# Another build-time order of the experts' steps in a two-block layer

## The chip, the cores and the metric

The kernel runs on one core of one Trainium2 chip. Times are device microseconds (us) of an execution; the median of three runs of the kernel before is 3551.99 us (3551.24 to 3552.19).

## The reference

`reference()` computes two transformer-like blocks one after the other on 1024 tokens of width 1024. The first has two linear-attention scans, and then a mixture of experts; the second has four mixers, a feed-forward layer and a gated projection. Only the mixture of experts matters here:

```python
def hier_moe(h, rg_w, rg_b, re_w, re_b, e_w_in, e_w_out):
    ...
    g_idx = jnp.argmax(g_logits, axis=-1)
    ...
    top_v, top_i = lax.top_k(e_in_group, TOP_K)
    weights = g_w * jax.nn.softmax(top_v, axis=-1)
    ...
    def expert_block(args):
        xb, e = args
        gate, up = jnp.split(xb @ e_w_in[e], 2, axis=-1)
        return (jax.nn.silu(gate) * up) @ e_w_out[e]
    ...
    y = yb[dest] * weights.reshape(-1)[order][:, None].astype(yb.dtype)
    out = jax.ops.segment_sum(y, token_of, num_segments=t)
```

32 experts share 2048 assignments of tokens. Each expert's weights are 6 MB in float32, 201 MB in all, and each is read once.

## The kernel before, in words

The routing sorts the experts by how many tokens they have got; what the program calls expert 0 is the one with most, up to 28, and the numbers 29 to 31 are three fixed experts. BLOCKS (line 21) gives each its blocks of rows: expert 0 has 128, 128, 128 and 64 rows, expert 1 has 128, 128 and 64, expert 2 has 128 and 64 (these three are the split experts), experts 3 to 7 have one block of 128 rows, 8 to 17 and 29 one of 64, and 18 to 28, 30 and 31 one of 32. There are 38 blocks. An expert's weights come in 12 chunks of 128 x 1024 (512 KB): eight for the first product, four for the second.

The blocks are shared out between two streams. The first stream has the list MANY (line 26). Its experts 0 to 7 use the fast float32r matmul with weights split in a high and a low part: a chunk is loaded into one of four places (tile `eraw`), split by ScalarE and VectorE into `ehi` and `elo` (`split`, lines 232 and 233) with twelve places each, and used by `block` (128 rows, six matmuls of 128 x 512 for each chunk, line 246) or `block_packed` (64 rows, line 1310). The weights of experts 30 and 29 are loaded ahead into the places of `ehi` and `elo`. The second stream has the list FEW (line 27): its chunks are loaded into one of ten places (tile `ew`) and used as they are, by `block_plain` (64 rows, lines 1358 to 1374) or `block_small` (32 rows, line 1399). Each block begins with a gather of its rows by GpSimd (`xg`, line 1238), a transposition by TensorE, and ends with a scatter (`y2d`, line 1427). Between the products ScalarE and VectorE compute silu and the product (`ga`), and their transposition (`ah`).

`blocks()` is a generator: for each step (a transposition, or the matmuls of one chunk or of two) it yields the planner's own length, the pause until the stream's next step can start, the chunks that the step needs, the expert, and whether this is the expert's last block. `run_experts()` is a planner that runs while the program is built. It keeps a time `t`, a bus on which a chunk takes TWELFTH and lands LANDING later, and for both streams the time at which their next step could start; it picks one step, lets the generator write its instructions, and goes on. When a step of an expert's last block has used its chunks, a place is free: for the second stream the next chunk's load is issued, for the first the place goes to a list and the next raw chunk that has landed is split into it, whereupon the next raw chunk is loaded. So the picks fix the order of all instructions of the stage on each engine, and the order of the loads on the DMA queue of SyncE, through which the 350 loads of the stage go (96 `eraw`, 254 `ew`; 34 more chunks are loaded ahead of it). At the end the order on each engine is made binding. In the kernel before a step of the second stream is taken if it can start no later than the first stream's, 0.05 us of play included. After the experts follow a loop for blocks that don't fit (zero passes here), and the next stage, which reads the scattered rows back from `y2d`.

Of the kernel before, what the change touches and what calls it, by code (L numbers as in the profile page):

```python
# [22 lines left out]
NB = sum(len(b) for b in BLOCKS)  # L23
NT = 64

MANY = (30, 29, 0, 1, 2, 3, 4, 5, 6, 7)
FEW = (31,) + tuple(range(8, 29))

PLACES = {"ew": 10, "ehi": 12, "elo": 12, "eraw": 4}
TWELFTH, LANDING = 1.45, 1.5  # L30

FIRST = (8, 10, 0, 12, 14, 4, -1, 1, 5, -2, 2, 6, 3, 7)

# [137 lines left out]
class Kern:  # L171
# [1295 lines left out]
    def run_experts(self, streams, orders, W, pools):  # L1467

        nc, tc = self.nc, self.tc
        cur = nc.cur_bb.bb
        first = len(cur.instructions)
        number, src = {}, lambda i, c: number[i](c)
        queue = [[(i, c) for i in o for c in range(12) if (i, c) not in W] for o in orders]
        there = {k: 0.0 for k in W}
        free, raws = [], []
        t, bus, cut, ready = 0.0, 0.0, 0.0, [0.0, 0.0]  # L1480

        def load(s):
            nonlocal bus
            if not queue[s]:
                return
            i, c = queue[s].pop(0)
            if i not in number:
                number[i] = self.expert(self.place(i))
            if s:
                w = W[i, c] = pools[1].tile([128, 1024], F32, tag="ew", name="ew", bufs=PLACES["ew"])  # L1490
                nc.sync.dma_start(w, src(i, c))
            else:
                w = pools[0].tile([128, 1024], F32, tag="eraw", name="eraw", bufs=PLACES["eraw"])
                nc.sync.dma_start(w, src(i, c))
            bus = max(t, bus) + TWELFTH
            if s:
                there[i, c] = bus + LANDING
            else:
                raws.append((i, c, w, bus + LANDING))

        def splits(now):

            nonlocal cut
            while raws and free and max(raws[0][3], free[0], cut) <= now:
                i, c, raw, at = raws.pop(0)
                cut = max(at, free.pop(0), cut) + 1.3
                hi, lo = [pools[0].tile([128, 1024], F32R, tag=n, name=n, bufs=PLACES[n]) for n in ("ehi", "elo")]
                self.split(hi, lo, raw)
                W[i, c] = hi, lo
                there[i, c] = cut + 1.3  # L1510
                load(0)

        for _ in range(PLACES["eraw"]):
            load(0)
        steps = [next(s, None) for s in streams]
        while any(steps):
            splits(t)
            at = [max([t, ready[s]] + [there.get((p[3], c), 1e9) for c in p[2]]) if p else 1e9 for s, p in enumerate(steps)]
            s = int(at[1] <= at[0] + 0.05)
            if at[s] > t + 0.25:  # L1520
                t += 0.2
                continue
            length, pause, cs, i, last = steps[s]
            t = max(t, at[s]) + length
            ready[s] = t + pause
            steps[s] = next(streams[s], None)
            for c in cs if last else ():
                if s == 1:
                    load(1)
                elif i < 8 or c % 2:  # L1530
                    free.append(t)
        assert not raws and not queue[0] and not queue[1]

        before = {}
        for ins in cur.instructions[first:]:
            if ins.engine in before:
                tc.add_manual_dep(ins, before[ins.engine], mybir.DependencyInfo(mybir.DependencyClass.NoSync, mybir.DependencyReason.DATA),
                                  reason="order of the experts")
            before[ins.engine] = ins.name

    def moe(self):
        nc, I, tc = self.nc, self.I, self.tc
        self.y2d = self.dr.tile([2048, 1024], F32, name="y2d")
        with ExitStack() as es:
            with ExitStack() as e1:
# [7 lines left out]
                with ExitStack() as e2:  # L1553
                    self.banks(e2, p=4)
                    self.route(self.pool(e2, "route", 1))
                    for e in (30, 29):
# [4 lines left out]
                self.tap("ord", self.ord)  # L1561
                streams = [self.blocks(pl, 1, [(i, j) for i in MANY for j in range(len(BLOCKS[i]))], W, "128"),
                           self.blocks(sm, 2, [(i, 0) for i in FEW], W, "64")]
                self.run_experts(streams, (MANY, FEW), W, (wp, sp))

# [819 lines left out]
```

## Time and profile before

| what | value |
|---|---|
| median of three runs | 3551.99 us |
| profiled execution, time | 3553.5 us |
| profiled execution, span | 3551.6 us |
| TensorE busy | 3315.7 us, 93% of the span |
| VectorE busy | 1836.0 us, 52% |
| ScalarE busy | 1141.1 us, 32% |
| GpSimd busy | 274.5 us, 8% |
| moved by DMA | 527.49 MB, 149 GB/s on the mean |
| mean granted clock of TensorE | 0.961 |

How to read it: the experts' stage lies from 805 us (the first load that the planner issues) to 1411 us. PE is TensorE, PEld its weight load, DVE VectorE, ACT ScalarE, POOL GpSimd, SP SyncE; L1399 is line 1399 of the kernel. A busy share that is an average over the span says little of one stage, so the rows below are of this stage. The granted clock is in parts of full speed.

### The profile page before, as it was taken

What the parts mean: (1) busy time and instruction counts of PE and PEld (TensorE: products, weight loads), DVE (VectorE), ACT (ScalarE), POOL (GpSimd) and SP (SyncE); (2) the same over time, 40 slices, a digit from 0 to 9 for tenths busy, and PEclk for the clock granted to TensorE, in tenths of its full rate; (3) what the DMA queues carried; (4) which work ended last, traced back from release to release, by engine and by line L of the source; (5) the groups of instructions that cost most, each with busy time, mean ns of one, the idle gap of its engine ahead of it and who ended that gap; (6) DMA issues with size and microseconds to landing.
All of it is one profiled execution on the core that took longest, in us unless ns stands there. A gap on an engine that the chain in (4) does not pass through costs nothing.

```text
span 3551.6 us, 42850 instructions
## 1 busy us (share of the span) xinstructions
PE 3315.7 (93%) x15995; PEld 2498.7 (70%) x15995; DVE 1836.0 (52%) x3311; ACT 1141.1 (32%) x2003; POOL 274.5 (8%) x246
## 2 busy tenths in 40 slices
PE   7999988986998886699999999999999999999998
PEld 4887767872444444477778777777787888888876
DVE  7846565773123455832355544556755444444455
ACT  2423242432112344522275223334314222212224
POOL 4001022002111110410000000000000000000000
PEclk8999978997999998799999999999999999999999
DMA  4234536359999986622221333324631111111122
GB/s 173 88 110 149 181 111 200 125 215 354 358 358 355 383 334 212 239 93 100 96 68 58 117 116 112 101 84 143 234 122 61 55 48 48 52 54 50 36 72 78
DMA packets 211723, 527.49 MB, mean 149 GB/s; under 512 B 22476, under 2 KB 72208, under 8 KB 209592
## 3 DMA queue, kind: packets, MB, share of 16 engines
q1 hardware_dynamic: 203704, 503.74, 40.1%
q0 software_dynamic: 6656, 16.79, 1.3%
q10 hardware_dynamic: 1152, 4.19, 0.3%
q8 instruction: 127, 2.08, 0.2%
q14 instruction: 84, 0.69, 0.1%
HBM read 445.43 MB, written 84.62 MB: 149 GB/s over the span
## 4 chain that ended last, share of the span: by engine, by line
PE 58%; DMA 3%; DVE 2%; ACT 1%; issue 1%; SPq 0%; POOL 0%; DVEq 0%; POOLq 0%; ACTq 0%
PE pd L239 8%; PE pd L240 8%; PE pd L238 8%; PE pg L238 5%; PE pg L239 5%; PE pg L240 5%; PE pp L239 3%; PE pp L240 3%; PE pp L238 3%; PE pS L1870 2%; PE po L1907 1%; DMA eraw<-in_ew 1%; PE pt L1894 1%; PE pg L246 1%; PE py L246 1%
## 5 line engine op out<-in xcount | busy, mean ns | idle before, releaser
L239 PE MATMUL pd<-H,thi 128*128 128x512 f32 x896 | 350.9, 392 | 0.5 <-DVE H L1649 0.5
L238 PE MATMUL pd<-H,thi 128*128 128x512 f32 x896 | 350.9, 392 | 0.1
L240 PE MATMUL pd<-H,tlo 128*128 128x512 f32 x896 | 350.7, 392 | 0.0
L232 ACT ACTIVATE thi<-traw 128x1024 fp32r<-128x1024 f32 (+3 forms) x145 | 132.5, 917 | 518.6 <-PE pd L239 319.0
L2257 DVE TENSOR_TENSOR M<-M,pp 128x512 f32<-128x512 f32 x256 | 173.8, 685 | 233.4 <-PE pp L240 232.4
L233 DVE TENSOR_TENSOR tlo<-traw,thi 128x1024 fp32r<-128x1024 f32 (+3 forms) x145 | 151.0, 1045 | 175.4 <-ACT thi L232 175.3
L238 PE MATMUL pg<-H,thi 128*128 128x512 f32 x512 | 209.4, 409 | 0.0
L240 PE MATMUL pg<-H,tlo 128*128 128x512 f32 x512 | 208.2, 407 | 0.0
L239 PE MATMUL pg<-H,thi 128*128 128x512 f32 x512 | 207.8, 406 | 0.0
L239 PE MATMUL pp<-flo,hh 128*128 128x512 f32 x512 | 199.2, 389 | 0.5 <-DVE flo L233 0.5
L238 PE MATMUL pp<-fhi,hh 128*128 128x512 f32 x512 | 199.4, 390 | 0.0
L239 PEld LDWEIGHTS pd<-H,thi 128*128 128x128 f32 x896 | 168.2, 188 | 41.7 <-issue 5.8
L238 PEld LDWEIGHTS pd<-H,thi 128*128 128x128 f32 x896 | 168.2, 188 | 39.0 <-issue 2.2
L240 PEld LDWEIGHTS pd<-H,tlo 128*128 128x128 f32 x896 | 168.2, 188 | 38.8 <-issue 4.3
L240 PE MATMUL pp<-fhi,hl 128*128 128x512 f32 x512 | 194.7, 389 | 0.0
L238 PE MATMUL pd<-nhi,mh 128*128 128x512 f32 x384 | 154.6, 404 | 4.5 <-ACT nhi L232 3.5
L239 PE MATMUL pd<-nlo,mh 128*128 128x512 f32 x384 | 153.1, 399 | 1.1 <-DVE nlo L233 1.1
L240 PE MATMUL pd<-nhi,ml 128*128 128x512 f32 x384 | 150.4, 401 | 0.0
L233 DVE TENSOR_TENSOR elo<-eraw,ehi 128x1024 fp32r<-128x1024 f32 x96 | 115.1, 1223 | 40.3 <-ACT ehi L232 39.2
L238 PEld LDWEIGHTS pg<-H,thi 128*128 128x128 f32 x512 | 96.4, 188 | 30.6 <-issue 9.6
L240 PEld LDWEIGHTS pg<-H,tlo 128*128 128x128 f32 x512 | 96.4, 188 | 25.9 <-issue 4.8
L239 PEld LDWEIGHTS pg<-H,thi 128*128 128x128 f32 x512 | 96.3, 188 | 25.6 <-issue 5.3
(764 smaller groups left out, 7156.6 us busy)
## 6 DMA issues: line engine op xcount, KB each, us to landing
ew<-in_ew SPq DMA_DIRECT2D x264, 512.0 KB
eraw<-in_ew SPq DMA_DIRECT2D x96, 512.0 KB
traw<-in_w2T SPq DMA_DIRECT2D x56, 512.0 KB
ada<-in_ada SPq DMA_DIRECT2D x64, 256.0 KB
gd<-sg SPq DMA_DIRECT2D x64, 256.0 KB
sg<-gd SPq DMA_DIRECT2D x64, 256.0 KB
traw<-in_ff1T SPq DMA_DIRECT2D x32, 512.0 KB
fraw<-in_ff SPq DMA_DIRECT2D x32, 512.0 KB
```

The source lines that it names most:

```text
L232: self.nc.scalar.activation(hi, src, AF.Copy)
L233: (eng or self.nc.vector).tensor_tensor(lo, src, hi.bitcast(F32), op=OP.subtract)
L238: mm(out, L[0], R[0], start=start, stop=False)
L239: mm(out, L[0], R[1], start=False, stop=False)
L240: mm(out, L[1], R[0], start=False, stop=stop)
L246: self.nc.tensor.matmul(out[j], L[a], R[b][:, j * 512:j * 512 + 512], start=start and i == 0, stop=stop and i == 2)
L1870: nc.tensor.matmul(p[:, :w], q[:, i * 128:i * 128 + 128], k[:, b * 512:b * 512 + w], start=True, stop=True)
L1894: nc.tensor.transpose(pt[:, j * 128:j * 128 + 128], P[:, jj * 128:jj * 128 + 128], self.ident)
L1907: nc.tensor.matmul(po[h * 64:h * 64 + 64, ii * 128:ii * 128 + 128], self.av[:, j, hh * 64:hh * 64 + 64], PT[:, j], start=(j == 0), stop=(j ...
L2257: nc.vector.tensor_tensor(X[:, t, c], X[:, t, c], p, op=OP.add)
```

## The change

The order of both lists changes: MANY now takes the large experts in the order 3, 0, 4, 5, 1, 6, 2, 7 and FEW takes a 64-row and a 32-row expert in turn. Where both streams' next steps can start within 0.05 us of each other, the first stream goes first if its step belongs to an expert's last block, otherwise the second; apart from that the earlier one goes, where the play of 0.05 us favoured the second stream. In the planner's own reckoning a step takes 1.08 of its length and a pause 1.15 of its own. The blocks, their instructions and their weights stay as they are.

```diff
--- before.py
+++ after.py
@@ -23,11 +23,12 @@
 NB = sum(len(b) for b in BLOCKS)
 NT = 64
 
-MANY = (30, 29, 0, 1, 2, 3, 4, 5, 6, 7)
-FEW = (31,) + tuple(range(8, 29))
+MANY = (30, 29, 3, 0, 4, 5, 1, 6, 2, 7)
+FEW = (31, 8, 18, 9, 19, 10, 20, 11, 21, 12, 22, 13, 23, 14, 24, 15, 25, 16, 26, 17, 27, 28)
+
 
 PLACES = {"ew": 10, "ehi": 12, "elo": 12, "eraw": 4}
-TWELFTH, LANDING = 1.45, 1.5
+TWELFTH, LANDING, SLOW = 1.45, 1.5, (1.08, 1.15)
 
 FIRST = (8, 10, 0, 12, 14, 4, -1, 1, 5, -2, 2, 6, 3, 7)
 
@@ -1470,6 +1471,7 @@
 
 
 
+
         nc, tc = self.nc, self.tc
         cur = nc.cur_bb.bb
         first = len(cur.instructions)
@@ -1516,13 +1518,15 @@
         while any(steps):
             splits(t)
             at = [max([t, ready[s]] + [there.get((p[3], c), 1e9) for c in p[2]]) if p else 1e9 for s, p in enumerate(steps)]
-            s = int(at[1] <= at[0] + 0.05)
+            s = int(at[1] < at[0])
+            if abs(at[1] - at[0]) < 0.05:
+                s = 1 - int(steps[0][4])
             if at[s] > t + 0.25:
                 t += 0.2
                 continue
             length, pause, cs, i, last = steps[s]
-            t = max(t, at[s]) + length
-            ready[s] = t + pause
+            t = max(t, at[s]) + length * SLOW[0]
+            ready[s] = t + pause * SLOW[1]
             steps[s] = next(streams[s], None)
             for c in cs if last else ():
                 if s == 1:
```

## Rows read from the trace of the kernel before

**Rows 1.** Page, part 2: 40 slices, TensorE's busy tenths and GB/s
```profile
PE   7999988986998886699999999999999999999998
GB/s 173 88 110 149 181 111 200 125 215 354 358 358 355 383 334 212 239 93 100 96 68 58 117 116 112 101 84 143 234 122 61 55 48 48 52 54 50 36 72 78
```

**Rows 2.** Stretches: us, busy us of five engines, TensorE's clock, DMA share, GB/s
```profile
820.00:1300.00 480.00, 426.56 (x2203) 213.90 (x2202) 163.02 (x218) 131.77 (x197) 71.40 (x66) 0.94 0.96 364
1300.00:1381.00 81.00, 55.44 (x230) 36.57 (x229) 53.36 (x54) 45.02 (x51) 8.98 (x6) 0.87 0.78 271
1381.00:1411.00 30.00, 26.02 (x103) 19.48 (x101) 8.77 (x10) 7.37 (x10) 2.00 (x1) 0.91 0.30 100
1300.00:1411.00 111.00, 81.46 (x331) 56.05 (x329) 62.13 (x64) 52.38 (x61) 10.98 (x7) 0.88 0.65 225
818.00:1411.00 593.00, 509.47 (x2544) 271.43 (x2544) 225.15 (x282) 184.54 (x258) 82.52 (x73) 0.93 0.90 337
```

**Rows 3.** SyncE's DMA queue: start, us, line, operation, out<-in, how many
```profile
804.92 4.05 SPq L1494 DMA_DIRECT2D eraw<-in_ew  x4
...
1298.26 0.91 SPq L1491 DMA_DIRECT2D ew<-in_ew  x2
1299.41 81.72 SPq L1494 DMA_DIRECT2D eraw<-in_ew  x39
```

**Rows 4.** The chain of waits near the end of the stage: start, us, what
```profile
1368.06 1.07 ACT ehi L232
1369.15 1.24 DVE elo L233
1370.40 5.10 DMA eraw<-in_ew
```

**Rows 5.** TensorE's waits, 1300 to 1411 us: us in total, times, longest
```profile
PE py L1277 <- DVE ga L1273: 10.6, 4, 5.7
PE py L246 <- ACT ah L232: 7.1, 3, 3.8
```

**Rows 6.** The page's third part, the queue of GpSimd's gathers and scatters
```profile
q0 software_dynamic: 6656, 16.79, 1.3%
```

**Rows 7.** Timeline of several engines, first and last pieces of the stage
```profile
818.55 1.88 PE L1390 MATMUL py<-ident,xg 32*128 32x32 f32 x16 [10.59 <-DMA xg<-h2d,gidx]
...
1304.56 1.06 PE L1399 MATMUL pg<-ew,xh 128*32 128x512 f32 x8
...
1310.79 3.14 PE L1399 MATMUL pg<-ew,ah 128*32 128x512 f32 x16 [1.81 <-DVE ah L1418]
1314.60 1.37 DVE L1423 TENSOR_TENSOR ey<-od,pg 32x512 f32<-32x512 f32 x2 [3.86 <-ACT od L1405]
...
1392.95 0.33 SPq L1673 DMA_DIRECT2D cx<-x1d  x1
...
1409.47 0.61 PE L246 MATMUL py<-ehi,al 128*128 128x512 f32 x2
1411.57 0.99 POOL L1427 DMA_INDIRECT y2d<-ey,sidx  x1 [21.91 <-DVEq L1573]
...
1432.72 1.97 PE L1643 MATMUL pp<-ident,cb 128*128 128x128 f32 x8 [22.63 <-DMA traw<-in_w2T]
```

**Rows 8.** A stretch of 20 us, the one with most traffic
```profile
1080.00:1100.00 20.00, 19.39 (x108) 11.05 (x108) 9.15 (x12) 7.61 (x11) 4.76 (x4) 1.00 1.03 410
```

**Rows 9.** Stretch of the tile ehi alone: ACT's count is the splits
```profile
820.00:1300.00 480.00, 158.27 (x478) 81.76 (x479) 66.84 (x56) 56.76 (x56) 0.94 0.96 364
```

**Rows 10.** TensorE's waits for split weights, 820 to 1300 us
```profile
PE pg L246 <- ACT ehi L232: 5.4, 3, 3.2
PE pg L246 <- DVE elo L233: 1.5, 3, 0.6
PE py L246 <- ACT ehi L232: 1.4, 1, 1.4
```

## The prediction

> **What bounds the kernel now.** I read the 40 slices of the page first [rows 1]. Two things stand beside each other from slice 10 to slice 15: the memory traffic is at its highest of the whole span (about 355 GB/s), and TensorE is nearly full too. That is the experts' stage, the only part that the change touches. So I next took the table of stretches for this stage [rows 2]. From 820 to 1300 us TensorE is busy for 426.56 of 480 us (0.889) while the DMA engines are busy at 0.96 and move 364 GB/s: both are close to full at once, and neither can give much. From 1300 to 1381 us both drop, TensorE to 55.44 of 81 us and the traffic to 271 GB/s; from 1381 to 1411 the traffic is 100 GB/s. The stage therefore has a long good part and 111 us of a poor end.
>
> The DMA queue of SyncE says why [rows 3]. The last weights of the second stream (FEW) are issued at 1298.26 us. From 1299.41 us on, 39 loads of the first stream (MANY) follow alone, and they need 81.72 us, 2.10 us each. Before that, 350 - 39 = 311 loads went out between 804.92 and 1299 us, 1.588 us each. A lone first stream is slow because each of its chunks is a chain of its own: the chain of waits shows a load, then a split on ScalarE (1.07 us), then one on VectorE (1.24 us), then the next load [rows 4], with four places for raw chunks. TensorE meanwhile waits for gated and transposed activations that stand behind those splits in the queues of ScalarE and VectorE, 10.6 + 7.1 us in this stretch [rows 5].
>
> **What the change does to the order.** The kernel's planner runs while the program is built, and its rule is short enough to be followed step by step. I used only the order that it gives, not its times. For the kernel before, the order ends with 39 raw loads in a row, which is just what the trace has [rows 3], so the rule is read rightly. With the new lists, tie rule and factors the same walk gives: expert 30 starts ahead of 31; the last raw load is number 340 of 350 and ten direct loads follow; expert 7 (the last of MANY) does its second product just after the first step of expert 28, the last of FEW, and the last seven steps of the stage are those of expert 28, a 32-row block; the last two loads, its own chunks, are issued when the first of these seven has freed two places. Before, 46 steps of the first stream followed the last step of the second; now none. Loads, matmuls, splits, gathers and scatters stay the same in number and size; only their order on each engine's queue, and on SyncE's, changes. The longest run of direct loads stays about as long (102 before, 100 now).
>
> **The sum.** Two terms carry it, and both lie on the path that sets the end of the stage.
> First, the 39 loads move into the mixed part. At its pace they cost 39 x 1.588 = 62 us, where they now take 81.7: 20 us less. Hence the last load goes out at 1299 + 62 = 1361 us. The same from the bytes: 350 loads of 0.524 MB are 183.5 MB, the gathers and scatters 16.8 MB [rows 6], together 200.3 MB; at 364 GB/s that is 550 us from 805, or 1355 us. The first is taken.
> Second, what follows the last load. Now a whole 128-row block does: the last load is issued at 1381.1 us and TensorE ends at 1410.1 us [rows 7], 29 us later. Afterwards it is the rest of a 32-row block: two steps of 1.06 us, and then what lies between the start of its fourth step at 1304.56 and the end of its last at 1313.93 us in expert 28 of the kernel before [rows 7], 9.4 us: 11.5 us in all. The landing (some 5 us by the last load's wait in the chain [rows 4]) is hidden under that. This is 17.5 us less, and TensorE ends near 1372.5 us.
> Against this, the 32-row block's way from TensorE to the scatter is ScalarE's od and two VectorE additions, which end 2.0 us after the matmuls, and then the issue; after the 128-row block the whole way was 1.5 us [rows 7]: about 1 us more. The next stage's TensorE start at 1432.72 [rows 7] hangs on weights issued behind the reading of the scattered rows, so it follows this end. Four prefetches of the next stage (the first at 1392.95 us [rows 7]) stand behind the experts' loads on SyncE; they were hidden under expert 7 and will be issued some 11 us ahead of the end. If that cover fails I allow 5 us, if the smaller scatter lands sooner -2 us, and I take zero, since the stage waits for the scatter anyhow. Starting with expert 30 in place of 31 is taken at zero: both wait for gathers issued one after the other, and the DMA engines are full there anyhow.
> The sum is -20 - 17.5 + 1 = -36.5 us. The profiled execution has a span of 3551.6 us and took 3553.5, 1.5 us above the median of the runs, 3551.99; so the median goes to 3515.
>
> **What could make it otherwise.**
> *TensorE sets the pace.* The new order needs TensorE's 509.47 us of this stage [rows 2] within 554 us, a share of 0.920, above the 0.889 of the good part. If it can't pass 0.889, the stage takes 509.47 / 0.889 = 573 us from 818.5 [rows 7] and ends at 1391, 19 us sooner than now: 3533. For it speaks that the good part holds idle time of TensorE (53 us) which mixing needn't remove; against it, that 509 us contain work at the lower clock (granted mean 0.88 from 1300 to 1411 against 0.94 before [rows 2]) which a fuller queue would shorten. A rule speaks against this rival: the Trainium skill, "Perfetto Trace Analysis", Identifying the Most-Contended Engine, holds that matmul busy time says little of how near TensorE is to its limit, and weight-load busy time more. By that, TensorE was loaded to only 213.90 of 480 us [rows 2], this rival would drop out, and the first sum would stand alone. I keep it, because the same rows show 53 us of open time and no more in which further matmuls could have started.
>
> *Both get better.* If the mixing holds places of both streams open all the time, the traffic could stay at the 410 GB/s that single stretches of 20 us show [rows 8]: 200.3 MB would need 489 us, and TensorE becomes the limit. With half of the good part's idle time gone it ends at 818.5 + 509 + 27 = 1354, -56 us: 3496. Against this the Trainium skill, "DMA: Bandwidth & Descriptors", Where 436 GB/s comes from, takes about 358 GB/s as what binds a core's transfers from HBM. By that figure, as an estimate, 200.3 MB need 560 us, the last byte lands at 1365 us and the sum stays near its -36. The stretch at 410 doesn't agree with such a bound; the mean of 364 does, so this rival keeps a small chance.
>
> *The splits hold up both streams (the other side).* All engines work their queue in order. The 40 splits that lie in the poor end now, where only their own stream suffers, move among the matmuls' evacuations of both streams: of 96 splits, 56 were in the good part [rows 9]. In the poor end TensorE stood idle 111 - 81.5 = 29.5 us beside 40 splits, 0.74 us each; in the good part its waits for split weights, 5.4 + 1.5 + 1.4 us [rows 10], make 0.15 us each for 56. If a split costs 0.74 us everywhere, TensorE needs 818 + 509 + 45 (the 53 us without those waits) + 96 x 0.74 = 1443 us, 33 us later than now: 3585. The point of no gain is at 0.40 us a split (38 us spare over 96), and the loss passes 0.2% from 0.47 us. For it: new ties go to the first stream, whose chunks come last. Against it: 0.15 us is what rows of mixed work show.
>
> *No change that can be told.* A split cost between those bounds, 0.33 to 0.47 us, or a tail that lengthens elsewhere by some 35 us. 3552.
>
> **How the numbers follow.** The DMA pace with the short tail, -36.5 us, has 0.45 (its own range 3504 to 3527: the byte sum's 6 us and as much again for loads that pack better on the one side; 5 us for the prefetches and 6 for a tail at the lower clock on the other). TensorE's pace, -19: 0.25. Both better, -56: 0.15. No change within 0.2% (7 us, about what a measurement can tell): 0.08. Slower through the splits: 0.07. So faster has 0.85, same 0.08, slower 0.07. The range leaves out the last two and a part of the best case, and reaches from -62 to -12 us: 3490 to 3540.
>
> **What would show it.** In the profile of the changed kernel the issues of both streams should end within some 15 us of each other, near 1361 us; no run of 39 raw loads; the last matmuls of the stage of the 32-row form, near 1372 us; the traffic at 355 to 375 GB/s up to the end, and TensorE above 0.9 busy. The first term is wrong if loads go out slower than 1.588 us each; the second, if another block ends last. If TensorE's waits for split weights come to more than 0.40 us a split, the other side was right; if TensorE stays below 0.9 while loads wait for places, its pace was the bound.

## The result, and the profile after

The changed kernel takes 3497.07 us (median of four runs, 3495.09 to 3499.05) where the kernel before takes 3552.09 us: a ratio of 0.9844, with a 95% interval of 0.9827 to 0.9861. That is 55 us sooner; the forecast was 37 us, with 3490 to 3540 as its range. The profiled execution has a span of 3493.3 us, 58.3 us less than that of before. Lines behind the edit have moved by one to four in `kernel.py`: line 1399 of before is 1400, 246 is 247, 1494 is 1496 and 1643 is 1647.

The page's slices, which answer to [rows 1]:

```profile
PE   7999988996998995899999999999999999999998
GB/s 176 78 111 154 187 93 212 121 186 341 382 389 378 397 383 281 181 97 97 76 79 64 121 136 91 95 82 190 201 109 73 49 49 49 49 51 49 33 73 79
```

The stretches of the experts' stage, to be held against [rows 2] (us, busy us of PE, PEld, DVE, ACT and POOL with counts, the granted clock, the DMA engines' share, GB/s):

```profile
820.00:1300.00 480.00, 436.67 (x2252) 233.44 (x2244) 197.16 (x245) 162.04 (x224) 69.97 (x64) 0.98 0.99 378
1300.00:1360.00 60.00, 49.62 (x272) 29.61 (x272) 27.46 (x36) 23.10 (x34) 6.74 (x7) 0.95 0.83 317
818.00:1360.00 542.00, 488.30 (x2531) 263.67 (x2529) 224.62 (x281) 185.53 (x258) 77.62 (x72) 0.97 0.97 370
```

The good part has become better and longer at once: 378 GB/s instead of 364 from 820 to 1300 us, and no poor end of 111 us behind it. All matmuls of the stage together are busy for 488.30 us instead of 509.47, since they run at the full clock more of the time (granted mean 0.97 instead of 0.93).

SyncE's queue at the end of the stage, which answers to [rows 3] (start, us, queue, line, operation, out<-in, how many):

```profile
1320.55 0.33 SPq L1496 DMA_DIRECT2D eraw<-in_ew  x1
1324.42 16.47 SPq L1493 DMA_DIRECT2D ew<-in_ew  x8
...
1349.06 0.93 SPq L1493 DMA_DIRECT2D ew<-in_ew  x2
...
1350.57 12.96 SPq L271 DMA_DIRECT2D nraw<-in_w2z  x2
```

The last raw load goes out at 1320.55 us and ten direct loads follow, as the walk through the planner's rule said. But the streams' last issues lie 28.5 us apart, where the prediction looked for some 15, and the traffic falls to 317 GB/s in the last 60 us, where it looked for 355 to 375 up to the end. TensorE's last pieces, which answer to [rows 7]:

```profile
1347.97 3.64 PE L1400 MATMUL pg<-ew,xh 128*32 128x512 f32 x32
1354.49 0.63 PE L1417 MATMUL py<-ident,ga 32*128 32x32 f32 x4 [2.88 <-DVE ga L1413]
1355.51 3.64 PE L1400 MATMUL pg<-ew,ah 128*32 128x512 f32 x16 [0.38 <-DVE cnt L1575]
1384.45 1.97 PE L1647 MATMUL pp<-ident,cb 128*128 128x128 f32 x8 [25.30 <-DVE cb L1713]
```

The stage ends with expert 28 at 1359.15 us, 51 us sooner. Split up, with the ends of the rows shown:

| stretch of the profiled execution | before, us | after, us | difference | forecast |
|---|---|---|---|---|
| up to the stage's first load | 804.9 | 803.8 | -1.1 | 0 |
| first load to the last load's issue | 576.2 | 546.2 | -30.0 | -20 |
| last load's issue to the experts' last matmul | 29.0 | 9.2 | -19.8 | -17.5 |
| to the next stage's first transposition | 22.6 | 25.3 | +2.7 | +1 |
| to line 1820 (1824 after), the first `av` | 148.2 | 139.8 | -8.4 | 0 |
| the rest | 1970.7 | 1969.0 | -1.7 | 0 |

The sum had -36.5 us, and the profiled execution lost 58.3. Of the 21.8 us between them, 10.0 lie in the loads' pace and 6.7 behind the experts' last matmul (8.4 less 1.7), in a stage that the change doesn't touch; the last block has 2.3, and 2.8 are in stretches for which nothing was forecast. Some 3 us of the 58.3 come from the executions that were profiled: that of before lies 1.4 us above the median of its runs, that of after 2.0 us below. The experiments went after the two large ones.

### The profile page after: what moved, and what is told of

It is laid out like the page before. It is cut to its first block, busy times and chain, and to the rows that moved or that the text cites. A ratio compares the mean times of both kernels' runs of the same rounds, so it can differ in the third digit from the quotient of the medians.

```text
span 3493.3 us, 42815 instructions
## 1 busy us (share of the span) xinstructions
PE 3295.4 (94%) x15995; PEld 2489.3 (71%) x15995; DVE 1833.0 (52%) x3311; ACT 1142.0 (33%) x2003; POOL 269.5 (8%) x246
## 3 DMA queue, kind: packets, MB, share of 16 engines
q1 hardware_dynamic: 203704, 503.74, 40.5%
## 4 chain that ended last, share of the span: by engine, by line
PE 57%; DVE 2%; DMA 1%; issue 1%; ACT 1%; POOL 0%; SPq 0%; DVEq 0%; POOLq 0%; ACTq 0%
PE pd L240 8%; PE pd L239 8%; PE pd L241 8%; PE pg L239 5%; PE pg L240 5%; PE pg L241 5%; PE pp L240 3%; PE pp L241 3%; PE pp L239 3%; PE pS L1874 2%; PE po L1911 1%; PE pt L1898 1%; PE pp L2125 0%; DMA nraw<-in_wpg 0%; DMA traw<-in_wbT 0%
## 5 line engine op out<-in xcount | busy, mean ns | idle before, releaser
L234 DVE TENSOR_TENSOR tlo<-traw,thi 128x1024 fp32r<-128x1024 f32 (+3 forms) x145 | 151.2, 1045 | 169.9 <-ACT thi L233 169.7
L239 PEld LDWEIGHTS pg<-H,thi 128*128 128x128 f32 x512 | 96.4, 188 | 30.6 <-issue 9.6
L233 ACT ACTIVATE ehi<-eraw 128x1024 fp32r<-128x1024 f32 x96 | 98.9, 1054 | 54.8 <-DMA eraw<-in_ew 34.7
```

The lines of the kernel that those rows point to most:

```text
L233: self.nc.scalar.activation(hi, src, AF.Copy)
L234: (eng or self.nc.vector).tensor_tensor(lo, src, hi.bitcast(F32), op=OP.subtract)
L239: mm(out, L[0], R[0], start=start, stop=False)
```

## The experiments

Each run has its own profile. Since the first load of the stage went out anywhere from 799.8 to 808.4 us in these profiles, though the program ahead of it is the same (but for e7, see there), I compare the *length* of the stage, from the first load's issue to the experts' last matmul: 605.2 us before and 555.4 after. "Together" is the part of it in which both streams still have steps, "alone" the rest. "Next" is from the experts' last matmul to line 1820, the first `av`. A length comes from one execution, and runs of one kernel differ by more than the small differences here: those of before on the chip of e1 to e4 reach from 3544.80 to 3557.07 us. So e1's and e2's 0.6 and 3.1 us aren't told from nothing by the lengths.

| kernel | ratio to before (95%) | stage | together, GB/s | alone | next |
|---|---|---|---|---|---|
| before | 1 | 605.2 | 509.0, 360 | 96.2, first stream | 170.8 |
| after | 0.9844 (0.9827 to 0.9861) | 555.4 | 544.2, 373 | 11.2, second | 165.1 |
| e1: lists | 1.0000 (0.9988 to 1.0011) | 604.6 | 534.8, 364 | 69.8, first | 170.5 |
| e2: tie rule | 0.9987 (0.9975 to 0.9999) | 602.1 | 539.9, 353 | 62.2, first | 169.4 |
| e3: lists, tie rule | 0.9927 (0.9898 to 0.9956) | 587.9 | 524.5, 351 | 63.4, second | 157.5 |
| e4: factors | 0.9981 (0.9967 to 0.9995) | 595.0 | 484.6, 369 | 110.4, first | 170.4 |
| e10: lists, factors | 0.9953 (0.9925 to 0.9980) | 584.6 | 489.9, 387 | 94.6, first | 171.0 |
| e8: after, old FEW | 0.9857 (0.9829 to 0.9886) | 567.8 | 564.9, 363 | 2.9, second | 162.8 |
| e9: after, old MANY | 0.9906 (0.9877 to 0.9934) | 571.6 | 536.9, 373 | 34.7, first | 169.9 |
| e11: other numbers | 0.9867 (0.9839 to 0.9896) | 564.5 | 561.6, 365 | 2.9, second | 163.9 |
| e12: larger factors | 0.9920 (0.9891 to 0.9949) | 581.0 | 578.0, 355 | 2.9, second | 163.2 |
| e6: two products | 0.9842 (0.9813 to 0.9870) | 549.4 | 539.4, 375 | 10.1, second | 166.1 |
| e7: more loads | 0.9964 (0.9945 to 0.9984) | 595.9 | 584.8, 387 | 11.1, second | 164.9 |
| e5: w2z late | 0.9896 (0.9867 to 0.9925) | 556.1 | 545.0, 373 | 11.1, second | 182.2 |

### The parts of the change, one by one

Theory A, from the prediction: the raw loads left alone and the block that ends last carry the gain. Its rivals let one part do the work by itself. The planner of the changed kernel was given back its old parts:

```diff
 # e1_lists: the new lists only; e3_lists_tie: the first line only
-TWELFTH, LANDING, SLOW = 1.45, 1.5, (1.08, 1.15)
+TWELFTH, LANDING, SLOW = 1.45, 1.5, (1.0, 1.0)
-            s = int(at[1] < at[0])
-            if abs(at[1] - at[0]) < 0.05:
-                s = 1 - int(steps[0][4])
+            s = int(at[1] <= at[0] + 0.05)
 # e2_tie: old lists, new tie rule, factors 1; e4_factors: old lists and tie rule, factors 1.08 and 1.15
-MANY = (30, 29, 3, 0, 4, 5, 1, 6, 2, 7)
...
+MANY = (30, 29, 0, 1, 2, 3, 4, 5, 6, 7)
+FEW = (31,) + tuple(range(8, 29))
```

> The new lists alone, with the old tie rule and factors of 1. Followed step by step, the order ends with 19 raw loads alone (39 before, none after) and a 128-row block last. Theory A (the lone run and the block that ends last carry the gain): 20 loads fewer alone at 2.10 - 1.56 = 0.54 us each, 11 us, and no gain at the end: the experts' last matmul near 1399 us (1410 before, 1359 after), 3541 us in all. Theory B (taking large and small experts in turn speeds the whole stage, whatever ends it): most of the 51 us come with the lists, last matmul at 1375 us or earlier, below 3520 us.

> The new tie rule alone, with the old lists and factors of 1. The order ends with 26 raw loads alone and a 128-row block last. Theory A: 13 loads fewer alone, 7 us, last matmul near 1403 us, 3545 us in all. Theory B (the lists do it): no change, 1408 to 1412 us, 3552 us.

> Lists and tie rule, with factors of 1: all of the change but the factors. No raw load is left alone; the order ends with 41 direct loads and 36 steps of the second stream alone. Theory A (only a lone first stream is slow): the same as the whole change, last matmul at 1359 us within 4, 3497 us. Rival (any stream that runs alone is slow, and the factors are there to end both together): 10 to 25 us later, 3507 to 3522 us.

> The planner's factors 1.08 and 1.15 alone, with the old lists and tie rule. The order ends with 46 raw loads alone and a 128-row block last. Theory A: 7 more loads alone than before, 4 us more, last matmul near 1414 us, 3556 us in all. Rival (the factors make the planned order fit the chip better, fewer waits of TensorE in the good part): 5 to 15 us sooner than before, 3537 to 3547 us.

Measured: the lists alone gave 3550.46 us (3549.38 for the kernel before on the same chip), the tie rule alone 3546.76, both together 3522.94, the factors alone 3545.24. The two parts of the stage, of before, of e1 and of e3 (columns as above; the first line of each pair has both streams together, the second one alone):

```profile
804.90:1313.90 509.00, 439.12 (x2282) 220.24 (x2279) 170.12 (x243) 135.94 (x204) 78.38 (x73) 0.93 0.95 360
1313.90:1410.10 96.20, 71.66 (x278) 52.08 (x276) 57.27 (x56) 48.58 (x56) 10.03 (x6) 0.87 0.66 226
```

```profile
804.20:1339.10 534.90, 467.90 (x2363) 234.25 (x2361) 195.45 (x264) 156.19 (x225) 81.01 (x75) 0.93 0.96 364
1339.10:1408.90 69.80, 50.32 (x190) 37.33 (x190) 32.76 (x35) 27.54 (x35) 5.80 (x5) 0.85 0.44 147
```

```profile
806.60:1331.10 524.50, 463.41 (x2334) 257.86 (x2333) 216.52 (x279) 175.41 (x246) 79.02 (x73) 0.95 0.93 351
1331.10:1394.50 63.40, 45.10 (x225) 13.11 (x224) 12.80 (x21) 11.85 (x18) 10.31 (x8) 0.84 0.95 371
```

Theory A holds for e2 alone (3545 us forecast). It gave e1 11 us that weren't there, e4 4 us more where 4.1 less were measured, and e3 the whole gain, of which half came. e1 has 20 raw loads fewer alone than before, yet gains next to nothing: the 19 that are left take 60.74 us, 3.2 us each, so the 2.10 us of the kernel before is not what a lone load costs everywhere. At the end of this order the splits that free the raw places wait, among other things, for matmuls of expert 2's last block (6.1 us). What is long is the row of *steps* left alone (36, for 69.8 us), not of loads. And e3 leaves no raw load alone, but 36 steps of the second stream, which take 63.4 us. TensorE is busy for 0.71 of them, and for 0.72 to 0.82 of the lone parts of the first stream; what differs is the traffic, 371 GB/s against 147 to 236. In before and e1 to e4 a lone step takes 1.76 to 2.09 us. The rival expected for e3, any lone stream is slow, came nearer than Theory A and missed by 1 us (3522.94 where it had 3507 to 3522). But e3 can be read otherwise. By its loads the lone second stream isn't slow, since 371 GB/s is what the change's mixed part moves (373). By bytes e3 loses in its mixed part: 351 GB/s instead of 373 over 524.5 us are 31 us, an estimate, of the 32.5 us that its stage is longer. These runs don't part the two readings, and they don't show why that mixed part moves less. e4 falls to its rival in time: with 8 steps more alone than before its stage is 10 us shorter and the runs' median 4.1 us, since its part together moves 369 GB/s instead of 360. That TensorE waits less there, as the rival had it, isn't seen: it is busy for 0.86 of that part in both.

From this came theory A2: the length is the steps of the mixed part times 1.186 us (with the factors; 1.215 to 1.246 without) and the lone steps times 2. It was tried on an order that hadn't run:

```diff
 # e10_no_tie: the changed kernel with the old tie rule
-            s = int(at[1] < at[0])
-            if abs(at[1] - at[0]) < 0.05:
-                s = 1 - int(steps[0][4])
+            s = int(at[1] <= at[0] + 0.05)
```

> New lists and factors with the old tie rule. Followed step by step, the order leaves 28 raw loads and 52 steps of the first stream alone at the end. Theory A2 (what the earlier runs left: a step of a stream that runs alone takes 2.0 us, a step of the mixed part 1.186 us where the factors are in and 1.215 to 1.246 where they are not): 402 x 1.186 + 52 x 2.03 = 582 us from 818, the last matmul at 1400 us, 3541 us in all. Rival (the lists and factors do it, the tie rule is a detail): within 10 us of the whole change, below 3508 us.

Measured: 3534.37 us, the experts' last matmul at 1389.8 us; from 818 us 477.2 us together, as worked out, and 94.6 alone instead of 105.6 (1.82 us a step). A2 is 10 us too long, its rival 26 us too short.

```profile
805.20:1295.20 490.00, 432.95 (x2269) 215.89 (x2266) 183.16 (x251) 148.21 (x212) 73.06 (x73) 0.95 1.01 387
1295.20:1389.80 94.60, 73.22 (x286) 54.77 (x286) 45.70 (x48) 38.77 (x48) 7.80 (x7) 0.87 0.47 161
```

The first line is the best mixed part of all orders, 387 GB/s, and the second the price: 161 GB/s for 94.6 us. So the tie rule earns its place by ending both streams together, not by a faster mixed part.

### What sets the pace of the mixed part

The loads or TensorE? One run takes work from TensorE, one adds loads.

```diff
 # e6_two_products
-        for i, (a, b) in enumerate(((0, 0), (0, 1), (1, 0))):
+        for i, (a, b) in enumerate(((0, 0), (0, 1))):
...
 # e7_more_loads, in load(), for each chunk
+            count[0] += 1
+            if count[0] % 5 == 0:
+                nc.sync.dma_start(pools[1].tile([128, 512], F32, tag="more", name="more", bufs=1), self.I["ew"][0, 0, :, :512])
             bus = max(t, bus) + TWELFTH
```

> The changed kernel without the third product (high weights by low activations) in the 128-row blocks of the first stream: 264 of its matmuls of 128 x 512 fewer, some 60 us of TensorE's work; loads, splits and the planned order stay. The loads set the pace: the experts' last matmul moves by 0 to 8 us from 1359 us. TensorE sets the pace: 40 to 60 us sooner, 1300 to 1320 us.

> The changed kernel with one more load of 256 KB, into a place that nobody reads, after each fifth load of the stage: 70 in all, 18.35 MB, 9% of the stage's bytes. The loads set the pace: 18.35 MB at 378 GB/s, 49 us later, the experts' last matmul near 1408 us, 3546 us in all. TensorE sets the pace: 0 to 15 us later, below 3512 us. Between the two: both are close to full, 25 to 40 us.

Measured: without the third product TensorE is busy for 31 us less (452.13 us of the mixed part, 483.43 after). That is less than the 60 us expected, and the granted mean fell from 0.96 to 0.93. The stage is 6.0 us shorter and ends at 1357.2 us; the whole takes 3498.22 us, no less than the change, since in this execution the first load went out 3.9 us later and what lies behind line 1820 took some 4 us more. With 70 loads more the stage is 40.5 us longer and the whole takes 3539.86 us. The mixed parts of after, e6 and e7:

```profile
803.80:1348.00 544.20, 483.43 (x2508) 264.19 (x2506) 225.04 (x293) 183.88 (x257) 82.51 (x77) 0.96 0.98 373
```

```profile
807.70:1347.10 539.40, 452.13 (x2245) 222.05 (x2246) 224.77 (x293) 183.65 (x257) 79.95 (x77) 0.93 0.99 375
```

```profile
804.90:1389.70 584.80, 500.52 (x2506) 266.91 (x2506) 225.81 (x293) 185.17 (x257) 80.19 (x77) 0.95 1.01 387
```

e7 added more than its text says. With the new place in the second stream's pool, the ten early loads of expert 31 went out inside the stage instead of ahead of it (the first row is of after, the second of e7):

```profile
756.59 5.48 SPq L1554 DMA_DIRECT2D ew<-in_ew  x10
809.89 16.32 SPq L1557 DMA_DIRECT2D ew<-in_ew  x10
```

So the stage has 23.6 MB more, not 18.35, which at 378 GB/s would be 62 us; two thirds of it are paid. The ten found room near the start, where the change moves only 67 GB/s from 819 to 824 us. Behind them, from the 31st to the 340th of the stage's own loads, the 62 added loads (16.3 MB, 43 us at 378 GB/s) cost 41 us. The loads set the pace: a fifth of the time that TensorE is busy less comes back, and once the stage is under way nearly all of what the added bytes cost is paid. The DMA engines weren't quite full all the same: with more loads queued they move 387 GB/s instead of 373. Nor is it the better granted clock that makes the change faster: e6 ran its mixed part at 0.93, as the kernel before did, and its stage is the shortest of all.

### Does an even end suffice?

In three more orders the streams end together, with three steps of one alone; in a fourth, e9, 19 steps of the first stream are left.

```diff
 # e8_many: the changed kernel with the old FEW; e9_few: with the old MANY
-FEW = (31, 8, 18, 9, 19, 10, 20, 11, 21, 12, 22, 13, 23, 14, 24, 15, 25, 16, 26, 17, 27, 28)
+FEW = (31,) + tuple(range(8, 29))
-MANY = (30, 29, 3, 0, 4, 5, 1, 6, 2, 7)
+MANY = (30, 29, 0, 1, 2, 3, 4, 5, 6, 7)
 # e11_even_end
-TWELFTH, LANDING, SLOW = 1.45, 1.5, (1.08, 1.15)
+TWELFTH, LANDING, SLOW = 1.35, 1.5, (1.0, 1.15)
 # e12_more
-TWELFTH, LANDING, SLOW = 1.45, 1.5, (1.08, 1.15)
+TWELFTH, LANDING, SLOW = 1.45, 1.5, (1.1, 1.3)
```

> The changed kernel with the old list FEW: all 64-row experts ahead of the 32-row ones. Followed step by step, the order ends with both streams together (3 steps of one alone). Theory A2 (what counts is how few steps a stream runs alone, 1.186 us a step in the mixed part with the factors): 451 x 1.186 + 8 = 543 us from 818, last matmul near 1361 us, 3499 us in all. Rival (taking 64-row and 32-row experts in turn is what keeps the loads even): 1375 us or later, above 3510 us.

> The changed kernel with the old list MANY: experts 0, 1 and 2 first. The order leaves 20 raw loads and 19 steps of the first stream alone. Theory A2: 435 x 1.186 + 19 x 1.9 = 552 us from 818, last matmul near 1370 us, 3508 us in all. Rival (taking large experts in turn matters by itself, alone steps or not): 1385 us or later, above 3522 us.

> Lists and tie rule of the change, but the planner's numbers are a bus time of 1.35 and factors 1.0 and 1.15 instead of 1.45, 1.08 and 1.15: in this order both streams end together too (3 steps of one alone), though the planner takes TensorE's steps and the bus to be faster than the chip's. Theory A2, even end: the last matmul within 8 us of the changed kernel's 1359 us, below 3506 us. Rival (the factors work because the planned times fit the chip's, which makes the mixed part faster): 1.227 us a step in the mixed part as with factors of 1, so 451 x 1.227 + 8 = 561 us from 818, 1379 us, 3517 us.

> The changed kernel with larger factors, 1.1 and 1.3; in this order both streams end together (3 steps of one alone). Theory A2 with the loads setting the pace: the same as the change within 6 us, 3491 to 3503 us. Rival (the nearer the planned times come to the chip's, the faster the mixed part): up to 10 us sooner, 3487 to 3491 us.

Measured: 3503.29, 3520.39, 3506.81 and 3525.46 us. By length, e8 is 12.4 us behind the change, e9 16.2, e11 9.1 and e12 25.6. A2 had e8, e11 and e12 within 8 us of the change, so it is too simple: orders that all end evenly differ by their mixed parts (355 to 373 GB/s). The rivals did no better: e8, e9 and e11 lie between A2 and theirs, and e12, with numbers still slower than the chip's, is the worst. No order was found that beats the change. The tie rule and the factors with both old lists weren't run, so what the lists add to those two is known only one list at a time.

e12 shows what such a loss looks like. Three stretches of its mixed part (columns as above):

```profile
1055.00:1080.00 25.00, 18.19 (x95) 10.29 (x92) 16.20 (x19) 14.24 (x20) 4.79 (x4) 0.86 0.79 297
1230.00:1255.00 25.00, 14.37 (x73) 8.27 (x72) 14.02 (x19) 12.82 (x18) 2.07 (x2) 0.73 0.91 360
905.00:1030.00 125.00, 116.61 (x643) 61.38 (x642) 26.96 (x45) 20.47 (x37) 16.90 (x19) 0.99 1.02 391
```

From 905 to 1030 us it runs as the change does there (391 GB/s; 393 in the changed kernel), but twice it falls back. In the second fall TensorE stops first, while the DMA engines still work off what was issued; their turn comes some 15 us later:

```profile
1235.00:1240.00 5.00, 0.63 (x4) 0.50 (x4) 2.00 (x3) 2.38 (x3) 0.00 (x0) 0.51 1.02 415
1250.00:1255.00 5.00, 3.78 (x29) 2.06 (x28) 3.77 (x6) 4.44 (x7) 2.07 (x2) 1.00 0.50 172
```

From 1230 to 1245 us the queues of ScalarE, VectorE and TensorE hold (start, us, engine, line, operation, tiles and, in brackets, idle time and its releaser):

```profile
1237.53 1.06 ACT L233 ACTIVATE ehi<-eraw 128x1024 fp32r<-128x1024 f32 x1 [2.26 <-DMA eraw<-in_ew]
1238.81 1.06 ACT L233 ACTIVATE ehi<-eraw 128x1024 fp32r<-128x1024 f32 x1 [0.23 <-DMA eraw<-in_ew]
1240.09 1.06 ACT L233 ACTIVATE ehi<-eraw 128x1024 fp32r<-128x1024 f32 x1 [0.22 <-DMA eraw<-in_ew]
1241.18 0.39 ACT L233 ACTIVATE ah<-py 128x256 fp32r<-128x256 f32 x1
```

```profile
1238.61 3.80 DVE L234 TENSOR_TENSOR elo<-eraw,ehi 128x1024 fp32r<-128x1024 f32 x3 [2.64 <-ACT ehi L233]
1242.33 0.42 DVE L234 TENSOR_TENSOR ah<-py,ah 128x256 fp32r<-128x256 f32 x1
1242.66 0.28 DVE L1419 COPY ah<-py 128x128 f32<-128x128 f32 x1
```

```profile
1236.03 0.63 PE L1417 MATMUL py<-ident,ga 32*128 32x32 f32 x4 [1.51 <-DVE ga L1413]
1242.99 1.93 PE L1400 MATMUL pg<-ew,ah 128*32 128x512 f32 x8 [6.33 <-DVE ah L1419]
```

ScalarE has reached splits whose raw chunks haven't landed yet (2.26 us of waiting, then one split after another as they come), and the `ah` of both streams stands behind them, in its queue and in VectorE's. TensorE waits 6.33 us for the second stream's, frees no place of that stream, and no direct load goes out from 1233.4 to 1244.9 us. This is the prediction's other side, at work in one order of the same steps. How much of e12's 25.6 us it is can only be bounded. In the changed kernel ScalarE waits for raw chunks in the mixed part too, 34.7 us, and the longest wait of TensorE for such an `ah` is 4.6 us; but it was 6.2 us in the kernel before, so one long wait is no mark of a bad order (who waits, tile and line, for what: us in all, how many waits, the longest; the last two lines are of before and of e12):

```profile
ACT ehi L233 <- DMA eraw<-in_ew: 34.7, 29, 4.5
```

```profile
PE pg L1400 <- DVE ah L1419: 13.8, 7, 4.6
PE pg L1399 <- DVE ah L1418: 11.3, 7, 6.2
PE pg L1400 <- DVE ah L1419: 21.9, 5, 6.3
```

TensorE is idle for 24 us more in e12's mixed part than in the change's. The waits for `ah` are 8.1 us of this; those for `ey` and `ga` in the queues of ScalarE and VectorE grew too, by 6.3 us (line 1391) and 6.0 us (line 1367). In the first fall it is an `ey` behind three splits of ScalarE for which TensorE waits 5.6 us. That the other waits stand behind splits too isn't shown.

### The stage behind the experts

> The changed kernel, but with the next stage's weights (w2z) loaded only after the first reading of the scattered rows. In the changed kernel two of its chunks are loaded at 1350 and 1363 us, and the time from the experts' last matmul to line 1820 of the kernel before is 165.1 us, 170.8 in the kernel before. Theory (this early load gave the 5.7 us between): the stretch goes back to 170 us or more and the whole to 3502 us or more, with the experts' last matmul at 1359 us within 3. Rival (another order of that stage's instructions, picked as the program is built, gave them): 165 us within 2, 3497 us.

```diff
 # e5_w2z_late, combine()
-                W = self.load_n(p0, I["w2z"][0], raw_bufs=1, bufs=4, engs=(nc.gpsimd, nc.gpsimd))
             for c in parts:
                 ld = nc.sync.dma_start(y[:, :, c], ...)
+            if t == 0:
+                with self.tc.issue_after(ld.ins):
+                    W = self.load_n(p0, I["w2z"][0], raw_bufs=1, bufs=4, engs=(nc.gpsimd, nc.gpsimd))
```

Measured: 3517.64 us; the stage is as long as in the change (556.1 us), and the stretch behind it takes 182.2 us instead of 165.1. The weights' chunks now go out at 1371.62 and 1385.08 us, and TensorE waits 7.5 us for them:

```profile
1355.44 0.43 SPq L286 DMA_DIRECT2D fg<-in_final_norm_g  x1
1370.38 1.19 SPq L1681 DMA_DIRECT2D y<-y2d  x2
1371.62 0.59 SPq L271 DMA_DIRECT2D nraw<-in_w2z  x1
...
1385.08 0.37 SPq L271 DMA_DIRECT2D nraw<-in_w2z  x1
```

```profile
PE pd L239 <- ACT nhi L233: 7.5, 2, 6.1
PE pd L240 <- DVE nlo L234: 3.2, 1, 3.2
```

What the theory forecast came true (170 us or more, 3502 us or more), but the loss is larger than the 5.7 us that it was to explain. In the kernel before the first of these chunks is issued 0.4 us ahead of the experts' last matmul, after a wait of 13.3 us for expert 7's last matmuls, so its place may be one that the first stream held:

```profile
SPq L270 <- PE py L246: 13.3, 1, 13.3
```

In the change the first stream ends 11 us ahead, so the chunk is loaded and split beside expert 28. The early load is worth something: TensorE's waits for the split chunks of w2z (`nhi` and `nlo`) come to 9.6 us in the kernel before, 0.5 in the change and 11.0 in e5. But e5's stretch is 11.4 us longer than that of before with nearly the same waits, so a large part of e5's loss isn't the late load. The order of the later instructions is chosen by a scheduler as the program is built, and it comes out otherwise when the stage ahead of it changes, in e5 as in the change; what it costs wasn't tried by itself. How much of the 5.7 us is that order and how much the early load, these runs don't tell; e3's 157.5 us are the shortest such stretch.

## Why the prediction was right, and where it was off

**The mechanism was right in the main.** The good part is bound by the loads, the poor end is one stream alone, and the change takes the poor end away. The walk through the planner's rule gave the order that the trace then showed (340th load the last raw one, seven steps of expert 28 last). e6 and e7 confirm the loads' pace, in the changed kernel; e10 confirms what a lone first stream costs. The price of the poor end by lone loads, 2.10 us each, was wrong beyond the order it was read from (e1).

**First term, -20 forecast, -30.0 measured.** The step "at its pace they cost 39 x 1.588 = 62 us" took the pace of the mixed part for fixed. It wasn't: the first 340 loads went out in 517.1 us, 1.521 us each, which is 23 us over 340 loads; the last ten, with few places free at the end, took 29 us and gave 13 of that back. The start, taken at zero because "the DMA engines are full there anyhow", wasn't free: they moved 67 GB/s from 819 to 824 us, and the 31st load went out 63.3 us after the first instead of 55.3. The factors have a part in this: e4 against before, and the change against e3, both have the faster mixed part. They aren't the whole of it, since e8 and e12, with factors, move 363 and 355 GB/s.

**Second term, -17.5 forecast, -19.8 measured.** The rest of a 32-row block took 9.2 us from the last issue instead of 11.5.

**The stage behind, +1 forecast, -5.7 measured** from the experts' end to line 1820. The prefetches were taken at zero, with -2 to 5 us as bounds; the first sum overlooked that a place of the first stream comes free earlier when the other stream ends last. TensorE's waits for the splits of these loads are 9.1 us shorter in the change than before. The premise of this term fell too: the next stage's first transposition was released by weights before (22.63 us, [rows 7]) and by `cb` after (25.30 us).

**The likeliest case's own range,** 3504 to 3527, missed the 3497.07 by 7 us; the wider range held it, because it reached towards the third case. So far the hit is luck: of the 21.8 us by which the profiled execution beat the sum, 12.3 are the sizes of its two large terms, and 9.5 lie where nothing or the opposite was forecast.

**TensorE's pace** (1391 us, -19) is refuted by e6. That its share in the mixed part is still 0.888 is no contradiction: 483.43 of 544.2 us are busy, but 31 us of that can go for a gain of 6. This bears out the rule weighed in the prediction: the Trainium skill, "Perfetto Trace Analysis", Identifying the Most-Contended Engine, on matmul busy time. The reason I gave for keeping the rival, that no more open time was left, was a misreading of a modelled busy time.

**Both better** (1354 us, -56) named the right total with a wrong reason: the traffic rose to 373 GB/s, not 410, and TensorE's idle time in the stage is 64 us (94 before), its busy time 20 us less. The 358 GB/s of the Trainium skill, "DMA: Bandwidth & Descriptors", Where 436 GB/s comes from, is not a bound here, with one core at work: e7 moved 387 GB/s over 585 us.

**The splits on the other side** did not decide the change, but the row named to watch for them was the wrong one. TensorE's waits for split weights are gone from the list after the change; the harm that was seen (e12) stood in the waits for `ah`, behind splits in the queues of ScalarE and VectorE.

## What to carry to other kernels

Where two streams of work share TensorE and the DMA engines, count the *steps* that one of them has left when the other ends, not only its loads: where 19 or more were left, each took here about 1.8 to 2.1 us instead of 1.2, whichever stream it was. Then look at which engine the lone stream leaves idle: only a lone first stream left the DMA engines idle, which set the pace. The numbers in a planner's model pay through the order that they bring about: lists, tie rule and factors gave 0.6, 3.1 and 10.2 us of stage one by one (by the runs' medians -1.1, 2.6 and 4.1) and 49.8 together, and slightly larger factors lost half of it, so such numbers have to be tried on the chip. And a stage's last holder of a place can decide when the next stage's first loads start.

## What the runs showed of the hardware that I had not expected

The traffic of loads of 512 KB doesn't stop at the 364 GB/s of the kernel before: 125 us of the changed kernel ran at 393 GB/s, with a DMA share of 1.03 (below). The one dip that was followed to its start, e12's second, came after 11.5 us in which no direct load went out.

```profile
905.00:1030.00 125.00, 116.81 (x622) 57.12 (x621) 26.30 (x44) 19.84 (x36) 17.14 (x18) 1.00 1.03 393
```
